# Seven-product pairs spread through each half of the down projection, post-norm transposes moved two kept tiles back, left operands built one block sooner

## The chip, the cores and the metric

The kernel runs on one core of a Trainium2 chip. The metric is the device time of one execution in microseconds (us), compared as the median of several runs. TensorE (PE in the tables) multiplies; VectorE (DVE) and ScalarE (ACT) prepare its operands; GpSimd (POOL) computes a few small things; SyncE (SP) issues nearly all weight loads.

## The reference

One layer of a decoder on an input `x` of 256 x 2048 in float32:

```python
h = x + 1/2 * post1(SwiGLU_1(pre1(x)))
u = pre_m(h);  p = u @ W_in          # S5 input, attention q/k/v, gates
h = h + post_m((sigmoid(g_A) * y_A + sigmoid(g_B) * y_B) @ W_out)
h = h + 1/2 * post2(SwiGLU_2(pre2(h)))

def _swiglu(x, wg, wu, wd):          # 2048 -> 5632 -> 2048
    return (jax.nn.silu(x @ wg) * (x @ wu)) @ wd
```

`pre` and `post` are RMS norms with a gain. `y_A` is a state-space branch, `y_B` a sparse attention. The change touches the two SwiGLU blocks, ffn1 and ffn2, and the norm behind ffn1.

## The kernel before

**Split products.** Every float32 operand is written as `hi + lo`, both rounded to the format that TensorE takes, and a product is three matmuls: hi by hi, lo by hi, hi by lo (lines 523 to 525; 278 to 280 in the plain blocks). A matmul is 128 x 128 by 128 x 512.

**Weight stream.** `Stream` loads weights as tiles of 128 x 1024 (512 KB): SP issues the load into one of `RAW_BUFS = 5` buffers (line 94), ACT makes `hi` (line 103), DVE makes `lo` (line 105). When DVE has made `lo`, the buffer is free and SP can issue the load five tiles on. DVE executes its instructions in program order.

**Seven-product pairs.** For some pairs of weight tiles, x and y, a 2 x 2 block product is done with seven products in place of eight (`fast_pair`): 21 matmuls in place of 24. DVE forms sums of x and y first: line 134 needs both tiles landed and writes the first half of `sums`, line 139 and line 140 write the second half. Then four operands are split: x itself, half of y (`ah0` in the down projection), the first half of the sums, and the second half. The last one is called *the last lo* here; its `lo` is read by the last product group of the pair. Line 139 of the next pair overwrites what the last lo reads.

**Left operands.** The activations have to be combined too (`fast_left_act`, lines 486 to 497: four sums, four differences, four splits of 128 x 384), once for ffn1, before block 5, and once for ffn2, before block 1, where the first seven-product blocks begin.

**Down projection.** `project` runs two halves of 1024 output columns. Within a half, `DOWN_MAIN` lists the order of the 18 pairs of weight tiles; 8 to 13 are seven-product pairs (`DOWN_FAST`), the others are plain pairs of 24 matmuls. Half 0 ends with pairs 18 to 21. In half 1 these four are kept: their eight split tiles stay in the buffer, are multiplied with the first 128 tokens (t = 0), then the post-norm of t = 0 runs (sum line 575, square line 390, scale line 400, power on POOL line 402, gain line 404, residual line 419, transposes line 322), and meanwhile the eight kept tiles are multiplied with the other 128 tokens (t = 1). `ORDER` places the transposes of t = 0 among these: before which kept tile stands which group.

```python
DOWN_FAST = (8, 9, 10, 11, 12, 13)
DOWN_MAIN = [0, 1, 2, 3, 8, 4, 9, 5, 6, 10, 7, 11, 14, 15, 12, 16, 13, 17]
ORDER = {3: 1, 4: 2, 5: 3}   # kept tile number: group of transposes
```

Of the kernel before, what the change touches and what calls it, by code (L numbers as in the profile page):

```python
# [22 lines left out]
KD = D // 128  # L23
# [11 lines left out]


DOWN_FAST = (8, 9, 10, 11, 12, 13)
DOWN_MAIN = [0, 1, 2, 3, 8, 4, 9, 5, 6, 10, 7, 11, 14, 15, 12, 16, 13, 17]
DOWN_ORDER = (DOWN_MAIN + [18, 19, 20, 21], DOWN_MAIN)
DOWN_KEPT = (18, 19, 20, 21)  # L40
RAW_BUFS = 5
# [6 lines left out]

EARLY_GATES = 3
OPENING = [(0, 0), 1, 2, (0, 1), (1, 0), 3, (0, 2), (1, 1), 4, (0, 3), (1, 2), (1, 3)]  # L50
ORDER = {3: 1, 4: 2, 5: 3}
MAGIC = 12582912.0
LN2_HI = 0.693359375
LN2_LO = -2.12194440e-4
# [119 lines left out]
def body(tc, a):  # L174
# [70 lines left out]
    stream = Stream(tc, st, items)  # L245
# [17 lines left out]
    background = []  # L263

    def pump(n=1):
        for _ in range(n):
            if background:
                background.pop(0)()

    def block(lhs, nk, width=512, tick=None, held=0, between=None, behind=None, lag=0):  # L270
        acc = [ps.tile([128, 512], F32, name="acc", tag="acc") for _ in range(NT)]

        def products(parts, kk, t):
            wh, wl = parts
            for k in range(wh.shape[1]):
                lh, ll = lhs(t, kk + k)
                o = acc[t][:, :width]
                T.matmul(o, lh, wh[:, k, :], start=kk + k == 0, stop=False)  # L278
                T.matmul(o, lh, wl[:, k, :], start=False, stop=False)  # L279
                last_product[0] = T.matmul(o, ll, wh[:, k, :], start=False, stop=kk + k == nk - 1).ins  # L280

        kk = 0
        kept = []
        late = []
        while kk < nk:
            parts = stream.next()
            products(parts, kk, 0)
            if kk < nk - held:
                late.append((parts, kk))
                if len(late) > lag:  # L290
                    products(*late.pop(0), 1)
            else:
                kept.append((parts, kk))
                if late:
                    products(*late.pop(0), 1)
            kk += parts[0].shape[1]
            if tick is not None:
                tick(kk)
        for x in late:
            products(*x, 1)  # L300
        if held:
            if between is not None:
                between(acc)
            for n, (parts, k0) in enumerate(kept):
                ins = behind(n) if behind is not None else None
                with tc.issue_after(ins) if ins is not None else nullcontext():
                    products(parts, k0, 1)
        return acc
# [126 lines left out]
    def project_plain(lhs, nk, post, held, tick=None):  # L435
        for nb in range(NBD):
# [5 lines left out]
            else:  # L442
# [7 lines left out]
                def behind(n):  # L450
                    c = ORDER.get(n)
                    return post.moved[0][c] if c is not None and post.moved[0] else None
# [46 lines left out]
    def fast_left_act(pool):  # L499
        step = 2 * (FAST_PAIRS[1] - FAST_PAIRS[0])  # L500

        def part(t, j):
            ks = slice(2 * FAST_PAIRS[0] + j, 2 * FAST_PAIRS[-1] + j + 1, step)
            return act_h[t][:, ks], act_l[t][:, ks]

        n = len(FAST_PAIRS)
        h, l = (pool.tile([128, 4, n, 128], F32R, name=nm) for nm in ("sh", "sl"))
        fast_left([(0, n, part)], lambda j, i, n: (h[:, j, i:i + n], l[:, j, i:i + n]))
        return lambda j, i: (h[:, j, i], l[:, j, i])
# [110 lines left out]
    def ffn(name, rr, gen, post, last, tables=False):  # L620
        g0 = first_block(name, gen) if gen is not None else opening(name)
        pools = []

        def open_pool(nm):
            pools.append(tc.tile_pool(name=nm, bufs=1, reuse_waits="tile"))
            return pools[-1].__enter__()

        hp = first_pool = open_pool("hTa")
        pre = [None]
        if tables:  # L630
            pre[0] = tc.tile_pool(name="pre", bufs=1, reuse_waits="tile")
            with tc.issue_after(stream.rounded[9]):
                s5_tables(pre[0].__enter__())
        hT = []
        pend = []

        def tick(kk):
            if kk == 8 and pend:
                pend.pop()()
            pump(1 + (kk % 8 == 0))  # L640

        def finish(nb, hs):
            def f():
                nonlocal hp
                if nb == 8:
                    hp = open_pool("hTb")
                x = hp.tile([128, NT, 2, 4, 128], F32R, name="hT", tag="hT", bufs=3 if nb >= 8 else 8)
                hT.append(x)
                for t in range(NT):
                    p = transpose4(hs[t])  # L650
                    S.activation(x[:, t, 0], p, AF.Copy)
                    V.tensor_tensor(x[:, t, 1], p, x[:, t, 0].bitcast(F32), op=ALU.subtract)
            return f

        fast = FAST_BLOCKS["ffn1" if tables else "ffn2"]
        left = None
        for nb in range(NBF):
            if nb in fast:
                if left is None:
                    if pre[0] is not None:  # L660
                        pump(len(background))
                        pre[0].__exit__(None, None, None)
                    fp = tc.tile_pool(name="fast", bufs=1, reuse_waits="tile")
                    stream.sums_pool = fp.__enter__()
                    left = fast_left_act(stream.sums_pool)

                def after(nb=nb):
                    if nb == fast[-1]:
                        fp.__exit__(None, None, None)
                        stream.sums_pool = None  # L670
                    if pend:
                        pend.pop()()

                banks = (xp, ps) if (nb - fast[0]) % 2 == 0 else (ps, xp)
                spare[0] = banks[1]
                g, u = both(left, *banks, after)
                spare[0] = xp
            else:
                g = g0 if nb == 0 else block(act, KD, tick=tick)
                u = block(act, KD, tick=lambda kk: pump(1 + (kk % 8 == 0)))  # L680
            hs = []
            for t in range(NT):
                sg = work()
                h = work()
                S.activation(sg, g[t], AF.Silu, scale=rr(t))
                V.scalar_tensor_tensor(h, u[t], rr(t), sg, op0=ALU.mult, op1=ALU.mult)
                hs.append(h)
            pend.append(finish(nb, hs))

        def lhs(t, kk):  # L690
            x = hT[kk // 4]
            return x[:, t, 0, kk % 4, :], x[:, t, 1, kk % 4, :]

        stream.alloc[last] = lambda: first_pool.tile(
            [128, NT, 2, 4, 128], F32R, name="hT", tag="hT", bufs=8).rearrange("p t h k c -> p (t h k c)")

        spaces = [ap_.tile([128, KD, 128], F32R, name=n, tag=n) for n in ("ah0", "al0", "ah1", "al1")]
        sums = spaces[1].bitcast(F32).rearrange("p (j k) c -> p j (k c)", j=4)
        stream.sums_pool = Spaces(spaces[0][:, :8].rearrange("p (j k) c -> p j (k c)", j=2), sums)
        n0 = DOWN_FAST[0] // 2  # L700

        def source(i, n):
            x = hT[n0 + i // 2]
            ks = lambda j: slice(2 * (i % 2) + j, 2 * (i % 2) + 2 * n, 2)
            return i, n, lambda t, j: (x[:, t, 0, ks(j)], x[:, t, 1, ks(j)])

        def place(j, i, n):
            if j == 2:  # L710
                return source(i, n)[2](1, 0)
            j = min(j, 2)
            if i == 5:
                return spaces[0][:, 8 + j:9 + j], spaces[0][:, 11 + j:12 + j]
            return tuple(x[:, 3 * i + j:3 * i + 3 * n - 2 + j:3] for x in spaces[2:])

        def dleft(j, i):
            return tuple(x[:, 0] for x in place(j, i, 1))

        gp = open_pool("gain")  # L720
        fast_left([source(0, 2)], place)
        gen2 = project(lhs, DOWN_ORDER, DOWN_KEPT, DOWN_FAST, dleft, post, (xp, ps), gp,
                       ({2: pend.pop(), 4: lambda: fast_left([source(2, 2)], place),
                         6: lambda: fast_left([source(4, 1), source(5, 1)], place)}, {}))
        stream.sums_pool = None
        for p in reversed(pools):
            p.__exit__(None, None, None)
        return gen2
# [755 lines left out]
```

## Time and profile before

| what | value |
|---|---|
| median of 3 runs | 2120.59 us (2119.51 to 2121.81) |
| profiled execution: its time, its span | 2119.69 us, 2117.9 us |
| outside the span | 1.8 us |
| PE busy | 2099.0 us, 99% of the span |
| DVE busy, ACT busy | 1576.2 us (74%), 1116.1 us (53%) |
| PE on the chain that ended last | 97% |

PE is the engine that sets the time, so the table of its few waits is the place to look for what can be won, and the slack between DVE and PE is the place to look for what can be lost.

### The profile page before, as it was taken

To read this page: it belongs to the slowest core of one execution; us is meant where nothing else is said; L and a number is where in the kernel's file an instruction comes from. 1 tells how busy PE (TensorE), PEld (TensorE's weight loads), DVE (VectorE), ACT (ScalarE), POOL (GpSimd) and SP (SyncE) were. 2 spreads that over 40 slices of the span, in tenths; PEclk is the share of its full clock that TensorE was granted. 3 is DMA by queue.
4 is the path that set the end of the run, shared out by engine and by line. 5 is a ranking of instruction groups with operands and counts; after the bars stand their busy time and mean duration, and the time that the engine had idled before them with its cause. 6 is when DMAs were issued, how large, how long until landed. Compare 5 with 4: busy or idle time off the path is not lost.

```text
span 2117.9 us, 27939 instructions
## 1 busy us (share of the span) xinstructions
PE 2099.0 (99%) x10048; PEld 1729.1 (82%) x10048; DVE 1576.2 (74%) x2268; ACT 1116.1 (53%) x1537; POOL 269.0 (13%) x494
## 2 busy tenths in 40 slices
PE   8999999999999999999999999999999999999998
PEld 7888788888888788998787778888888888888886
DVE  7998898986867864455466656567998899778676
ACT  6444455554555565554445554465555555555453
POOL 1222200000000002993104320000000000000000
PEclk9999999999999999999999999999999999999999
DMA  8877666665665756567854346675666665656665
GB/s 285 269 244 248 191 207 206 193 217 173 215 208 192 271 194 224 166 217 257 276 164 139 123 144 211 209 268 166 212 189 195 201 210 181 218 170 209 218 208 179
DMA packets 137146, 437.63 MB, mean 207 GB/s; under 512 B 14880, under 2 KB 27312, under 8 KB 136880
## 3 DMA queue, kind: packets, MB, share of 16 engines
q1 hardware_dynamic: 117504, 403.10, 59.1%
q10 hardware_dynamic: 19504, 32.75, 4.6%
q8 instruction: 79, 1.29, 0.2%
q14 instruction: 59, 0.48, 0.1%
HBM read 417.42 MB, written 21.52 MB: 207 GB/s over the span
## 4 chain that ended last, share of the span: by engine, by line
PE 97%; DMA 1%; issue 1%; DVE 0%; ACT 0%; POOL 0%; DVEq 0%; SPq 0%; POOLq 0%; ACTq 0%
PE bank L523 16%; PE bank L524 16%; PE bank L525 16%; PE acc L278 14%; PE acc L279 14%; PE acc L280 14%; PE xp L322 2%; PE xp L1262 1%; PE xp L989 1%; DMA raw<-in_w_in 1%; PE xp L1250 1%; PE xp L1012 1%; PE xp L1151 0%; PE xp L1226 0%; PE xp L1227 0%
## 5 line engine op out<-in xcount | busy, mean ns | idle before, releaser
L105 DVE TENSOR_TENSOR lo<-raw,hi 128x1024 fp32r<-128x1024 f32 (+3 forms) x676 | 797.4, 1190 | 353.5 <-ACT hi L103 343.4
L103 ACT ACTIVATE hi<-raw 128x1024 fp32r<-128x1024 f32 (+3 forms) x676 | 685.6, 1023 | 635.8 <-PE acc L280 340.6
L278 PE MATMUL acc<-hi,ah 128*128 128x512 f32 (+2 forms) x1072 | 415.3, 389 | 1.9 <-ACT hi L103 1.9
L279 PE MATMUL acc<-lo,ah 128*128 128x512 f32 (+2 forms) x1072 | 414.4, 387 | 0.0
L280 PE MATMUL acc<-hi,al 128*128 128x512 f32 (+2 forms) x1072 | 413.1, 386 | 0.0
L524 PE MATMUL bank<-lo,ah 128*128 128x512 f32 x758 | 296.8, 392 | 0.0
L525 PE MATMUL bank<-hi,al 128*128 128x512 f32 x746 | 290.9, 390 | 0.0
L523 PE MATMUL bank<-hi,ah 128*128 128x512 f32 x758 | 274.6, 392 | 1.0 <-ACT hi L103 1.0
L278 PEld LDWEIGHTS acc<-hi,ah 128*128 128x128 f32 x1072 | 201.6, 188 | 42.6 <-ACT hi L103 2.7
L279 PEld LDWEIGHTS acc<-lo,ah 128*128 128x128 f32 x1072 | 201.8, 188 | 38.6 <-issue 1.9
L280 PEld LDWEIGHTS acc<-hi,al 128*128 128x128 f32 x1072 | 201.7, 188 | 37.9 <-issue 0.2
L524 PE MATMUL bank<-lo,hT 128*128 128x512 f32 x520 | 202.7, 390 | 0.0
L525 PE MATMUL bank<-hi,hT 128*128 128x512 f32 x520 | 202.6, 390 | 0.0
L523 PE MATMUL bank<-hi,hT 128*128 128x512 f32 x520 | 191.0, 390 | 0.1
L523 PEld LDWEIGHTS bank<-hi,ah 128*128 128x128 f32 x758 | 141.3, 188 | 31.8 <-ACT hi L103 3.4
L524 PEld LDWEIGHTS bank<-lo,ah 128*128 128x128 f32 x758 | 142.4, 188 | 29.6
L525 PEld LDWEIGHTS bank<-hi,al 128*128 128x128 f32 x746 | 140.2, 188 | 28.7
L103 ACT ACTIVATE hi<-sums 128x1024 fp32r<-128x1024 f32 x84 | 89.0, 1059 | 125.8 <-DVE sums L140 109.4
L105 DVE TENSOR_TENSOR lo<-sums,hi 128x1024 fp32r<-128x1024 f32 x84 | 102.8, 1224 | 35.0 <-ACT hi L103 35.0
L523 PEld LDWEIGHTS bank<-hi,hT 128*128 128x128 f32 x520 | 97.5, 188 | 20.9 <-ACT hi L103 0.9
L525 PEld LDWEIGHTS bank<-hi,hT 128*128 128x128 f32 x520 | 97.6, 188 | 20.3
L524 PEld LDWEIGHTS bank<-lo,hT 128*128 128x128 f32 x520 | 97.7, 188 | 20.2
(322 smaller groups left out, 2679.6 us busy)
## 6 DMA issues: line engine op xcount, KB each, us to landing
raw<-in_ffn_gu SPq DMA_DIRECT2D x352, 512.0 KB, 4.1
raw<-in_ffn_d SPq DMA_DIRECT2D x176, 512.0 KB, 4.3
raw<-in_w_ya SPq DMA_DIRECT2D x64, 512.0 KB, 3.5
raw<-in_w_in SPq DMA_DIRECT2D x40, 512.0 KB, 4.3
raw<-in_w_gate_b SPq DMA_DIRECT2D x32, 512.0 KB, 4.2
raw<-in_w_out SPq DMA_DIRECT2D x32, 512.0 KB, 4.1
raw<-in_w_o SPq DMA_DIRECT2D x16, 512.0 KB, 3.7
tab<-s5out ACTq DMA_DIRECT2D x8, 768.0 KB, 5.9
```

What stands on the lines that cost most here:

```text
L103: self.rounded.append(nc.scalar.activation(h, r, AF.Copy).ins)
L105: self.rest = nc.vector.tensor_tensor(l, r, h.bitcast(F32), op=ALU.subtract).ins
L278: T.matmul(o, lh, wh[:, k, :], start=kk + k == 0, stop=False)
L279: T.matmul(o, lh, wl[:, k, :], start=False, stop=False)
L280: last_product[0] = T.matmul(o, ll, wh[:, k, :], start=False, stop=kk + k == nk - 1).ins
L322: last_transpose[0] = T.transpose(p[:, k, :], src[:, k * cols:(k + 1) * cols], ident).ins
L523: T.matmul(out, lh, wh[:, j, :], start=key not in self.started, stop=False)
L524: T.matmul(out, lh, wl[:, j, :], start=False, stop=False)
L525: last_product[0] = T.matmul(out, ll, wh[:, j, :], start=False, stop=last).ins
L989: T.matmul(sp[:, r, q, :], bt[:, r, q, :], urel[:, ct, q, :], start=True, stop=True)
L1012: T.matmul(yps[-1][64 * q2:64 * q2 + 64, ct % 2, qh, :], st8[:, r, 4 * ct + q, 0:64] if r < 2 else urel[:, ct, q, :], tab[:, r, q, :], sta ...
L1250: T.transpose(p[:, b, kb, :], PP[:, hf, b, kb * 128:(kb + 1) * 128], ident)
```

## The change

Three edits. `DOWN_MAIN` now alternates seven-product and plain pairs one by one. `ORDER` puts the transposes before kept tiles 5, 6 and 7 in place of 3, 4 and 5; the mixer's output projection reads the same table. The left operands of the first seven-product block are built in the up product of the block ahead of it, at its fifth step (`kk == 4`), not at the block's own start.

```diff
-DOWN_MAIN = [0, 1, 2, 3, 8, 4, 9, 5, 6, 10, 7, 11, 14, 15, 12, 16, 13, 17]
+DOWN_MAIN = [0, 1, 2, 3, 8, 4, 9, 5, 10, 6, 11, 7, 12, 14, 13, 15, 16, 17]
-ORDER = {3: 1, 4: 2, 5: 3}
+ORDER = {5: 1, 6: 2, 7: 3}
@@ ffn
-                if left is None:
-                    if pre[0] is not None:
-                        pump(len(background))
-                        pre[0].__exit__(None, None, None)
-                    fp = tc.tile_pool(name="fast", bufs=1, reuse_waits="tile")
-                    stream.sums_pool = fp.__enter__()
-                    left = fast_left_act(stream.sums_pool)
...
-                u = block(act, KD, tick=lambda kk: pump(1 + (kk % 8 == 0)))
+                def tick_u(kk, nb=nb):
+                    nonlocal left, fp
+                    pump(1 + (kk % 8 == 0))
+                    if nb + 1 == fast[0] and kk == 4:
+                        if pre[0] is not None:
+                            pump(len(background))
+                            pre[0].__exit__(None, None, None)
+                        fp = tc.tile_pool(name="fast", bufs=1, reuse_waits="tile")
+                        stream.sums_pool = fp.__enter__()
+                        left = fast_left_act(stream.sums_pool)
+
+                u = block(act, KD, tick=tick_u)
```

Both programs have the same instructions, only in another order. On DVE, in half 0 of ffn1's down projection, behind pair 8 (its last lo reads `al0_4724`, where the sums lie), before:

```order
755 L140 TENSOR_TENSOR al0_4724<-al0_4724,raw_4896 128x512
756 L105 TENSOR_TENSOR lo_5059<-al0_4724,hi_5058 128x1024
757 L105 TENSOR_TENSOR lo_5069<-raw_4955,hi_5068 128x1024
758 L105 TENSOR_TENSOR lo_5078<-raw_4967,hi_5077 128x1024
759 L105 TENSOR_TENSOR lo_5088<-raw_4980,hi_5087 128x1024
760 L105 TENSOR_TENSOR lo_5100<-raw_4998,hi_5099 128x1024
761 L134 TENSOR_TENSOR al0_4724<-raw_5056,raw_5072 128x1024
```

and now:

```order
755 L140 TENSOR_TENSOR al0_4724<-al0_4724,raw_4896 128x512
756 L134 TENSOR_TENSOR al0_4724<-raw_4980,raw_4998 128x1024
757 L105 TENSOR_TENSOR lo_5057<-al0_4724,hi_5056 128x1024
758 L105 TENSOR_TENSOR lo_5067<-raw_4955,hi_5066 128x1024
759 L139 TENSOR_TENSOR al0_4724<-al0_4724,raw_4980 128x512
760 L105 TENSOR_TENSOR lo_5076<-raw_4967,hi_5075 128x1024
761 L105 TENSOR_TENSOR lo_5089<-raw_4980,hi_5088 128x1024
```

The tiles raw_4980 and raw_4998 were two plain tiles and are now a seven-product pair, so line 134, which needs both landed, stands ahead of the last lo of the pair before (lo_5059, now lo_5057), where nothing stood.

In half 1 of the same projection, on DVE from the first place where the two orders differ, before:

```order
841 L105 TENSOR_TENSOR lo_5906<-al0_4724,hi_5905 128x1024
842 L105 TENSOR_TENSOR lo_5924<-al0_4724,hi_5923 128x1024
843 L105 TENSOR_TENSOR lo_5934<-raw_5860,hi_5933 128x1024
844 L105 TENSOR_TENSOR lo_5943<-raw_5872,hi_5942 128x1024
845 L105 TENSOR_TENSOR lo_5953<-raw_5885,hi_5952 128x1024
846 L134 TENSOR_TENSOR al0_4724<-raw_5921,raw_5937 128x1024
847 L105 TENSOR_TENSOR lo_5965<-raw_5903,hi_5964 128x1024
```

and now, one whole turn of a seven-product pair and a plain pair:

```order
842 L134 TENSOR_TENSOR al0_4724<-raw_5885,raw_5903 128x1024
843 L105 TENSOR_TENSOR lo_5922<-al0_4724,hi_5921 128x1024
844 L139 TENSOR_TENSOR al0_4724<-al0_4724,raw_5885 128x512
845 L105 TENSOR_TENSOR lo_5932<-raw_5860,hi_5931 128x1024
846 L140 TENSOR_TENSOR al0_4724<-al0_4724,raw_5903 128x512
847 L105 TENSOR_TENSOR lo_5941<-raw_5872,hi_5940 128x1024
848 L105 TENSOR_TENSOR lo_5954<-raw_5885,hi_5953 128x1024
849 L105 TENSOR_TENSOR ah0_4723<-raw_5903,ah0_4723 128x512
850 L105 TENSOR_TENSOR lo_5984<-al0_4724,hi_5983 128x1024
851 L134 TENSOR_TENSOR al0_4724<-raw_5963,raw_5981 128x1024
852 L105 TENSOR_TENSOR lo_6000<-al0_4724,hi_5999 128x1024
```

Again line 134 has moved ahead of a last lo (lo_5924, now lo_5922), and in this half it does so in two turns running; raw_5981 is loaded into the buffer that lo_5954 frees.

On PE, at the end of ffn1, the place of the transposes of t = 0 (xp), before:

```order
3113 L524 MATMUL bank_5696<-hT_6375,hT_4826 128x512
3114 L525 MATMUL bank_5696<-hT_6375,hT_4826 128x512
3115 L322 MATMUL xp_6509<-ident_75,wk_5485 128x128 x4
3116 L322 MATMUL xp_6524<-ident_75,wk_5487 128x128 x4
3117 L523 MATMUL bank_5696<-hT_6400,hT_4826 128x512
```

and now:

```order
3125 L524 MATMUL bank_5697<-hT_6411,hT_4482 128x512
3126 L525 MATMUL bank_5697<-hT_6411,hT_4482 128x512
3127 L322 MATMUL xp_6509<-ident_75,wk_5413 128x128 x4
3128 L322 MATMUL xp_6524<-ident_75,wk_5415 128x128 x4
3129 L523 MATMUL bank_5697<-hT_6422,hT_4482 128x512
3130 L322 MATMUL xp_6539<-ident_75,wk_6278 128x128 x4
3131 L322 MATMUL xp_6554<-ident_75,wk_6280 128x128 x4
```

The transposes stand two kept tiles (twelve matmuls) later, and the third and fourth group follow the first two with one matmul between.

## Rows read from the trace of the kernel before

**Rows 1.** The page: busy time, share of the span and instructions of each engine.

```profile
PE 2099.0 (99%) x10048; PEld 1729.1 (82%) x10048; DVE 1576.2 (74%) x2268; ACT 1116.1 (53%) x1537; POOL 269.0 (13%) x494
```

**Rows 2.** A wait of PE in the whole span: total us, times, longest.

```profile
PE bank L523 <- ACT hi L103: 1.0, 4, 0.3
```

**Rows 3.** Timeline of PE, block 5 of ffn1: start, length, instruction, idle before.

```profile
260.79 0.39 PE L524 MATMUL bank<-lo,sh 128*128 128x512 f32 x1
261.47 0.51 PE L523 MATMUL bank<-hi,ah 128*128 128x512 f32 x1 [0.29 <-ACT hi L103]
261.81 0.39 PE L525 MATMUL bank<-hi,sl 128*128 128x512 f32 x1
...
264.15 0.40 PE L525 MATMUL bank<-hi,al 128*128 128x512 f32 x1
```

**Rows 4.** Timelines of PE, DVE and POOL at ffn1's post-norm.

```profile
732.71 0.39 PE L525 MATMUL bank<-hT 128*128 128x512 f32 x1
735.15 1.78 PE L322 MATMUL xp<-ident,wk 128*128 128x128 f32 x8 [2.05 <-DVE wk L419]
...
731.34 0.68 DVE L575 TENSOR_TENSOR wk<-bank,wk 128x512 f32<-128x512 f32 x1
...
734.34 1.42 DVE L419 SCALAR_TENSOR_TENSOR wk<-wk,rpa 128x512 f32<-128x512 f32 x2 [0.46 <-POOL rpa L402]
```

**Rows 5.** Windows: PE, PEld, DVE, ACT, POOL busy (instructions), PE clock, DMA share, GB/s.

```profile
205.00:247.00 42.00, 42.00 (x214) 34.11 (x213) 30.12 (x48) 18.01 (x20) 14.60 (x32) 1.00 0.73 229
1416.00:1440.00 24.00, 24.00 (x108) 19.88 (x107) 9.95 (x11) 10.12 (x10) 0.00 (x0) 1.00 0.45 151
735.20:739.00 3.80, 3.80 (x14) 3.09 (x15) 2.50 (x5) 3.64 (x12) 0.00 (x0) 0.55 0.97 356
```

**Rows 6.** Timeline of DVE: four full-wide lo behind each other.

```profile
544.28 4.63 DVE L105 TENSOR_TENSOR lo<-raw,hi 128x1024 fp32r<-128x1024 f32 x4
```

**Rows 7.** Timeline of PE: first product with the last lo, in the four halves.

```profile
544.56 0.39 PE L524 MATMUL bank<-lo,ah 128*128 128x512 f32 x1
...
659.05 0.39 PE L524 MATMUL bank<-lo,hT 128*128 128x512 f32 x1
...
659.96 0.39 PE L524 MATMUL bank<-lo,ah 128*128 128x512 f32 x1
...
1913.81 0.39 PE L524 MATMUL bank<-lo,ah 128*128 128x512 f32 x1
...
2029.20 0.39 PE L524 MATMUL bank<-lo,ah 128*128 128x512 f32 x1
```

**Rows 8.** Single loads: when SP issued them, and us to landing.

```profile
L94 SPq DMA_DIRECT2D raw<-in_ffn_d x1: 327/327/327, 539.0 to 539.0; - x1
DMA to landing us min/median/max: 4.7/4.7/4.7
...
L94 SPq DMA_DIRECT2D raw<-in_ffn_d x1: 446/446/446, 653.3 to 653.3; - x1
DMA to landing us min/median/max: 4.8/4.8/4.8
...
L94 SPq DMA_DIRECT2D raw<-in_ffn_d x1: 328/328/328, 1908.2 to 1908.2; - x1
DMA to landing us min/median/max: 4.5/4.5/4.5
...
L94 SPq DMA_DIRECT2D raw<-in_ffn_d x1: 327/327/327, 2022.2 to 2022.2; - x1
DMA to landing us min/median/max: 4.9/4.9/4.9
```

**Rows 9.** All weight loads of half 0 and of half 1: us to landing.

```profile
DMA to landing us min/median/max: 3.4/4.4/5.5
...
DMA to landing us min/median/max: 3.3/4.5/6.0
```

**Rows 10.** Waits for loads in the seven-product blocks of ffn1, 262 to 440 us.

```profile
  DVE sums L134: 1.8, 2
```

More of the change, by code (lines that the diff above doesn't have):

```diff
@@ L655, in ffn @@
         fast = FAST_BLOCKS["ffn1" if tables else "ffn2"]
-        left = None
+        left = fp = None
         for nb in range(NBF):
             if nb in fast:
-                if left is None:
-                    if pre[0] is not None:
-                        pump(len(background))
-                        pre[0].__exit__(None, None, None)
-                    fp = tc.tile_pool(name="fast", bufs=1, reuse_waits="tile")
-                    stream.sums_pool = fp.__enter__()
-                    left = fast_left_act(stream.sums_pool)
                 def after(nb=nb):
```

## The prediction

> **What bounds the kernel now.** I read the busy times first: PE works in 99% of the span [rows 1], so the time changes only by work taken off PE, which this change doesn't do, by waits of PE, or by its clock. The list of PE's waits and the starts of its matmuls then show what there is to win: a new matmul starts every 0.227 us when nothing is late (659.05 to 659.96 is four of them) [rows 7].
>
> Three places lose time that the change speaks to. In block 5 of ffn1, 8 steps of PE take from 260.79 to 264.15, 3.36 us, where 8 x 0.227 = 1.81 would do: 1.55 us lost, because ACT's hi comes late [rows 3]. The list counts four such waits, two here and two in block 1 of ffn2, so I take 1.55 us twice [rows 2]. At ffn1's post-norm the last kept product of the first stretch starts at 732.71 and the first transpose at 735.15, 2.44 us where 0.23 would do: 2.21 us [rows 4]. Behind it PE ran at a mean clock of 0.55, so at the lower of its two levels, 1.2 GHz, nearly throughout 735.2 to 739 [rows 5]; that costs (1 - 0.55) x 3.8 = 1.7 us more. All told 1.55 + 1.55 + 2.2 + 1.7 = 7.0 us.
>
> **The left operands.** The four sums, four differences and four low parts (twelve DVE instructions, about 0.55 us each) and ACT's four splits move one block ahead. They are some 6 us of DVE. From 205 to 247, where they now fall, DVE is busy 30.12 of 42 us, and from 1416 to 1440 for ffn2 9.95 of 24 [rows 5]: 12 and 14 us are free, so they fit, and DVE and ACT no longer have them in front of the splits that PE waits for. I take both 1.55 us as won. If they only half fit, the bounds are 0 and 3.1 us.
>
> **The transposes.** Before, three kept tiles (18 matmuls) lay behind the last t = 0 product of the row sum; now five do. Two tiles are 12 x 0.227 = 2.72 us of cover; the wait was 2.2 us [rows 4]. Of the chain, the last sum (line 575, at 731.34) came late behind a lo and the chain from it to line 419 took 3.0 us; in the new order the lo stands earlier and the loads of the residual are issued before the kept tiles' loads, so the chain starts no later. Cover exceeds need by 0.5 us at least, and with no idle there is nothing to halve the clock: 3.9 us won. The later transposes delay the next projection's first products by nothing that the cover doesn't hold; at the mixer PE waits for no transpose before, and I put the edit there at nothing.
>
> **The pairs.** Moving them removes no work. What moves is line 134: on DVE it now waits for the second tile of the next pair, ahead of the last lo of the present pair, and everything on DVE queues behind it. PE reads that lo in its next products. So the last lo is ready one line 134 and one lo behind the landing: 1.14 + 1.22 [rows 6], with 0.1 for the signals 2.5 us. Until there nothing has moved, so the landing times of before hold. The four halves [rows 7, 8]:
>
> ffn1 half 0: issued 539.0, landed 543.7, lo ready 546.2, read at 544.56: 1.65 us late.
> ffn1 half 1: 653.3, 658.1, 660.6, read at 659.96: 0.65 us late.
> ffn2 half 0: 1908.2, 1912.7, 1915.25, read at 1913.81: 1.45 us late.
> ffn2 half 1: 2022.2, 2027.1, 2029.65, read at 2029.20: 0.45 us late.
>
> This repeats, because pairs now alternate. A turn of a seven-product pair and a plain pair is 45 matmuls, 10.2 us of PE. On DVE, where a last lo stands behind line 134, the turn is, from line 134's start: last lo at 1.1, line 139 at 2.4, a plain lo at 3.0, line 140 at 4.1, a second plain lo at 4.7, the lo of x at 5.9, done at 7.1 (full-wide 1.14 us apart, half-wide about half). Only then is x's buffer free, and SP issues the next pair's second tile into it. I price its landing at 4.5 us, the median of the loads in these halves (3.3 to 6.0 [rows 9]); there are others in flight 1 and 3 us ahead of it, so the lone load's 3.4 is too short and 4.8 the other end. With 0.1 the turn is 11.75 us, 1.55 over PE's. In the second place of half 1 this comes on top in full: 0.65 + 1.55 = 2.2 us late. Where the last lo stands ahead of line 134, the turn is 10.5 to 10.6 us and what comes late is the first plain lo, by 0.2 to 0.5 us. Carried through in this way, half 0 of ffn1 loses 1.65 + 0.25 = 1.9, half 1 loses 0.65 + 1.55 + 0.45 + 0.4 = 3.05; ffn2 1.45 + 0.25 = 1.7 and 0.45 + 1.55 + 0.45 + 0.4 = 2.85. That is 9.5 us in some 12 waits; and the matmul behind a wait starts 0.34 us, not 0.23, after the last (261.47 to 261.81) [rows 3], so 12 x 0.11 = 1.3 more. Loss 10.8 us. With a landing of 3.4 in the later turns it would be 1.65 + 1.2 + 1.45 + 1.0 and 6 waits, 6.0 us; with 4.8 about 14.
>
> The Trainium skill, page "DMA: Bandwidth & Descriptors", section "Anatomy of one DMA — SWDGE (gpsimd) path", gives a load as about 2.0 us plus its bytes over 436 GB/s. By it 512 KB would land in 3.2 us, an estimate, and the loss would be about 5.5 us; the loads here come from SP's queue, and their shortest of 3.3 and median of 4.4 to 4.5 [rows 9] are what the sum uses.
>
> **The sum.** 10.8 - 7.0 = 3.8 us over the profiled execution's 2119.69: 2123.5. That execution was 0.9 us below the median of the three runs, so on the median it is 2124.4 us, 0.18% up. A measurement of this kernel tells some 0.2% (4.2 us) from no change, so this is just within.
>
> **The rivals.**
> The clock falls too. The one idle of PE that was followed by the lower clock was 2.05 us [rows 4]; those of 0.3 us in block 5 were not. The new ones of 1.45 to 1.65 us, one in each half, lie between, and nearer to the first. One fall costs 1.7 us, but DVE's turn catches up meanwhile, so that later waits in that half vanish: net 1.5 in half 0, 0.9 in half 1. All four: 4.8 us on top, 2129.2; one or two: 2126. The Trainium skill, page "TensorE: Matmul & The Clock Gate", section "HAM oscillation — how this bites in real kernels", tells of a loop whose matmuls wait for a load in each turn and lose the clock in each turn; the fall at 735 us is a case of it here, but after one wait and with 2.05 us of idle.
>
> Only the first waits count: the later second tiles land like lone loads, in 3.4 us. Loss 6.0, 2119.6 us on the median, no change.
>
> Faster: no new wait of weight. The seven-product blocks of ffn1 alternate in the same way, and there line 134 waited twice, 1.8 us in all, in 180 us [rows 10], without PE. Against it: there line 134 stands behind the last lo and one plain lo. It decides at the landing: if each second tile, the first ones too, landed in 3.4 us, the first waits would be 0.35 and 0.3 us, the others none, and nearly the whole 7.0 us were won: 2114.3 us. No load that counts was that fast.
>
> The change does little of what it says: the left operands meet other work and the 3.1 us stay: 2127.
>
> **How the numbers follow.** Forecast 0.47, with its own range 2121.5 to 2127 (landings of 4.1 to 4.8 us). Clock 0.25, first waits only 0.13, faster 0.11, operands late 0.04. Slower by over 0.2% is the clock's 0.25, a third of the forecast's and the last case's 0.04, less a little: 0.42. Faster 0.11, and the rest 0.47. The range holds 8 in 10 only with one of the two ends; since both have weight I go from 2114 to 2129.
>
> **What would show it.** Right: waits of PE for DVE's lo in the down projections, at about 543, 657, 668 us and their like in ffn2, the first some 1.6 us; DVE's line 134 idle before it, released by a load; no wait in block 5 of ffn1 and block 1 of ffn2; no idle and no lower clock at the transposes. Wrong: lower clock behind those waits (the clock's rival), waits in the second turns below 1 us (short landings), or a transposes' wait that is only moved.

## The result and the profile after

The changed kernel is slower by more than the prediction's whole range allowed: median 2133.86 us of six runs (2129.38 to 2138.06), beside 2121.78 us for the kernel before (six runs on the same chip), ratio 1.0059 with a 95% interval of 1.0044 to 1.0073. That is 12.1 us, where 3.8 were forecast. The profiled execution of the changed kernel took 2138.06 us (span 2136.2) and was the slowest of its six; that of before, 2119.69 us, was on the quick side of its own. Between the two traces there are thus 18.4 us to be placed, and the account below is made for these; the medians are accounted for separately at the end.

The busy line of the page answers to [rows 1]:

```profile
PE 2102.0 (98%) x10048; PEld 1727.5 (81%) x10048; DVE 1571.7 (74%) x2268; ACT 1115.7 (52%) x1537; POOL 272.2 (13%) x494
```

The work is the same; what grew is waiting. The list of PE's waits in the changed kernel (line waited on, total us, times, longest) holds three rows that the one of before doesn't have: the first, the fourth and the last one below. The row of [rows 2] and the wait for line 419 are gone from it:

```profile
PE bank L524 <- DVE lo L105: 15.1, 14, 2.4
PE xp L322 <- DMA wk<-in_x: 5.3, 2, 5.1
PE acc L278 <- ACT hi L103: 1.9, 2, 1.4
PE xp L322 <- DVE bd L862: 1.9, 1, 1.9
PE xp L1017 <- POOL st L1005: 1.2, 1, 1.2
```

The same matmul can be looked up in both traces; the difference of its two start times says how far the changed kernel has fallen behind by then. The places where this difference jumps give the account (us, worked out from the starts of PE's rows in the two traces):

```
place (us in the trace before)              forecast   measured
start of the kernel                            0         +0.56
226: transposes line 322 wait for bd           0         +2.16
262-268: block 5 of ffn1                      -1.55      -1.35
272, 314, 402: ffn1's seven-product blocks     0         +3.77
ffn1 half 0: four waits                       +1.9       +5.44
ffn1 half 1: a wait and the clock behind it   +3.05      +4.40
735-746: transposes of the post-norm          -3.9       -3.95
973: line 1017 waits for POOL                  0         +1.30
1463: block 1 of ffn2                         -1.55      -1.57
ffn2 half 0: two waits                        +1.7       +2.89
ffn2 half 1: four waits                       +2.85      +4.52
```

The rows sum to 18.2 us; the forecast for the halves had 1.3 us more for restarts, spread over its waits.

The three gains came out to within 0.2 us. PE's timeline in the changed kernel shows the transposes starting 0.23 us behind the kept product, where [rows 4] had 2.44 us, and a window over them (columns as in [rows 5]) has the full clock, where that had 0.55:

```profile
750.54 0.39 PE L525 MATMUL bank<-hT 128*128 128x512 f32 x1
750.77 1.03 PE L322 MATMUL xp<-ident,wk 128*128 128x128 f32 x8
```

```profile
748.00:752.00 4.00, 4.00 (x24) 3.38 (x24) 3.45 (x9) 3.66 (x12) 0.42 (x1) 1.00 0.73 255
```

The losses came where the prediction put them, and larger. In half 0 of ffn1 PE's timeline has four of them (in brackets the idle time ahead and what ended it), where a first of 1.65 us and small ones of 0.25 us together were forecast:

```profile
551.29 0.50 PE L524 MATMUL bank<-lo,ah 128*128 128x512 f32 x1 [1.46 <-DVE lo L105]
...
563.65 0.50 PE L524 MATMUL bank<-lo,hT 128*128 128x512 f32 x1 [0.26 <-DVE lo L105]
...
575.78 0.50 PE L524 MATMUL bank<-lo,hT 128*128 128x512 f32 x1 [1.63 <-DVE lo L105]
...
587.01 0.50 PE L524 MATMUL bank<-lo,hT 128*128 128x512 f32 x1 [0.95 <-DVE lo L105]
```

On DVE, in half 1, the cause stands as the prediction described it: line 134 sits idle until a load lands, and the last lo (`lo<-al,hi`) is queued directly behind it. Between two such stops DVE does its whole turn in one run:

```profile
668.14 1.23 DVE L134 TENSOR_TENSOR al<-raw 128x1024 f32<-128x1024 f32 x1 [3.28 <-DMA raw<-in_ffn_d]
669.28 1.22 DVE L105 TENSOR_TENSOR lo<-al,hi 128x1024 fp32r<-128x1024 f32 x1
670.54 0.69 DVE L139 TENSOR_TENSOR al<-al,raw 128x512 f32<-128x512 f32 x1
...
675.76 1.21 DVE L105 TENSOR_TENSOR lo<-al,hi 128x1024 fp32r<-128x1024 f32 x1
681.08 1.23 DVE L134 TENSOR_TENSOR al<-raw 128x1024 f32<-128x1024 f32 x1 [4.11 <-DMA raw<-in_ffn_d]
682.23 1.22 DVE L105 TENSOR_TENSOR lo<-al,hi 128x1024 fp32r<-128x1024 f32 x1
```

The run frees four buffers in 3.5 us, so SP issues four loads close together, at 575.8, 577.5, 578.6 and 579.2 in half 0. The first is alone and takes 3.5 us; the third is the second tile y that line 134 waits for; the fourth takes longest. Three views of SP's loads of that turn: all four, the third and the fourth.

```profile
L94 SPq DMA_DIRECT2D raw<-in_ffn_d x4: 328/328/328, 575.8 to 579.2; - x4
...
DMA to landing us min/median/max: 3.5/5.2/6.5
...
L94 SPq DMA_DIRECT2D raw<-in_ffn_d x1: 328/328/328, 578.6 to 578.6; - x1
...
DMA to landing us min/median/max: 5.8/5.8/5.8
...
L94 SPq DMA_DIRECT2D raw<-in_ffn_d x1: 328/328/328, 579.2 to 579.2; - x1
...
DMA to landing us min/median/max: 6.5/6.5/6.5
```

So y lands 5.8 us after its issue, not 4.5; line 134 is late, DVE's next run is bunched again, and the burst repeats itself. From one line 134 to the next, half 0 takes 12.36, 11.40 and 11.96 us (548.88, 561.24, 572.64, 584.60), where PE needs 10.2 and the prediction had 10.5 to 10.6 for this half.

What the prediction had no term for is the stretch at 226 us, ahead of block 5, where the left operands now lie. Rows of POOL, DVE, ACT and PE of the changed kernel there:

```profile
212.53 6.80 POOL L892 COPY hz<-hs 32x32 f32<-32x32 f32 x1 [13.95 <-DVE hs L887]
...
219.18 1.28 DVE L652 TENSOR_TENSOR hT<-xp,hT 128x512 fp32r<-128x512 f32 x2
...
224.50 2.01 ACT L103 ACTIVATE hi<-raw 128x1024 fp32r<-128x1024 f32 x2 [7.99 <-POOL hz L892]
...
225.59 1.22 DVE L105 TENSOR_TENSOR lo<-raw,hi 128x1024 fp32r<-128x1024 f32 x1 [4.80 <-ACT hi L103]
...
228.10 0.63 PE L322 MATMUL xp<-ident,bd 128*128 128x128 f32 x4 [1.89 <-DVE bd L862]
```

A tiny copy of 32 x 32 on POOL takes 6.80 us. In the trace of before the same copy takes 0.51:

```profile
208.78 0.51 POOL L887 COPY hz<-hs 32x32 f32<-32x32 f32 x1 [14.67 <-DVE hs L882]
```

It is the first of sixteen such copies, and ACT issues the DMA that sends out their result behind the last of them. All sixteen and that issue, first in the changed kernel, then before:

```profile
212.53 11.48 POOL L892 COPY hz<-hs 32x32 f32<-32x32 f32 x16 [13.95 <-DVE hs L887]
...
224.04 0.34 ACTq L896 DMA_DIRECT2D s5out<-hz  x1
...
208.78 8.70 POOL L887 COPY hz<-hs 32x32 f32<-32x32 f32 x16 [14.67 <-DVE hs L882]
...
217.51 0.34 ACTq L891 DMA_DIRECT2D s5out<-hz  x1
```

So ACT issues it 6.5 us later. Only 2.8 us of these are the longer copies; the other 3.75 us are their later start: they wait for line 887 on DVE, which now stands behind work of the left operands (the whole kernel was 0.6 us behind by then). ACT stands 7.99 us in front of this DMA, its next hi comes late, DVE waits 4.80 us for that hi, and PE's transposes wait 1.89 us for DVE.

### The profile page after: what moved, and what is told of

It reads as the page before. It is cut to its first block, busy times and chain, and to the rows that moved or that the text cites. A ratio compares the mean times of both kernels' runs of the same rounds, so it can differ in the third digit from the quotient of the medians.

```text
span 2136.2 us, 27921 instructions
## 1 busy us (share of the span) xinstructions
PE 2102.0 (98%) x10048; PEld 1727.5 (81%) x10048; DVE 1571.7 (74%) x2268; ACT 1115.7 (52%) x1537; POOL 272.2 (13%) x494
## 4 chain that ended last, share of the span: by engine, by line
PE 74%; DVE 9%; POOL 7%; DMA 5%; issue 3%; ACT 1%; DVEq 0%; SPq 0%; ACTq 0%; POOLq 0%
PE bank L524 12%; PE bank L525 11%; PE acc L278 11%; PE acc L279 11%; PE acc L280 11%; PE bank L523 11%; DVE lo L105 5%; DMA raw<-in_ffn_d 4%; PE xp L322 2%; POOL st L1005 2%; POOL sc L1002 2%; POOL sc L1003 1%; POOL st L1004 1%; DMA raw<-in_ffn_gu 1%; POOL hz L892 1%
## 5 line engine op out<-in xcount | busy, mean ns | idle before, releaser
L105 DVE TENSOR_TENSOR lo<-raw,hi 128x1024 fp32r<-128x1024 f32 (+3 forms) x676 | 797.3, 1186 | 349.5 <-ACT hi L103 345.1
L524 PE MATMUL bank<-lo,ah 128*128 128x512 f32 x758 | 297.6, 393 | 9.6 <-DVE lo L105 9.6
L523 PE MATMUL bank<-hi,ah 128*128 128x512 f32 x758 | 281.4, 391 | 0.0
L524 PE MATMUL bank<-lo,hT 128*128 128x512 f32 x520 | 203.8, 392 | 5.5 <-DVE lo L105 5.5
L524 PEld LDWEIGHTS bank<-lo,ah 128*128 128x128 f32 x758 | 142.4, 188 | 42.5 <-DVE lo L105 13.9
L524 PEld LDWEIGHTS bank<-lo,hT 128*128 128x128 f32 x520 | 98.0, 188 | 28.8 <-DVE lo L105 8.6
L105 DVE TENSOR_TENSOR lo<-sums,hi 128x1024 fp32r<-128x1024 f32 x84 | 101.0, 1216 | 5.1 <-ACT hi L103 4.3
```

What stands on the lines that cost most here:

```text
L105: self.rest = nc.vector.tensor_tensor(l, r, h.bitcast(F32), op=ALU.subtract).ins
L523: T.matmul(out, lh, wh[:, j, :], start=key not in self.started, stop=False)
L524: T.matmul(out, lh, wl[:, j, :], start=False, stop=False)
```

## The experiments

Each experiment was timed beside the kernel before, whose median lay between 2121.3 and 2121.9 us throughout.

**ORDER alone, pairs alone, left operands alone.** Three kernels each make one of the three edits of the diff: its line of `ORDER`, its line of `DOWN_MAIN`, its piece in `ffn`. The expectations:

> Only the transposes' table is changed, the other two edits are left as before. Theory (the five-tile cover hides the whole chain of the post-norm): no wait at ffn1's transposes, no lower clock behind them, 3.9 us less than before, ratio about 0.998. Rival (with the DVE order of before, line 575 still comes late behind a lo, and the wait is only moved to the fifth kept tile): at most 1 us won, ratio 0.9995 or more, and a wait of PE for line 419 stays in the list.

> Only the order of the pairs in the down projections is changed. Theory (the alternating pairs alone make the last lo late, by landings of 5 to 6 us of each pair's second tile): 10 to 17 us more than before, ratio 1.005 to 1.008, some ten waits of PE for DVE's lo in the four halves, none before 530 us; the profiled runs of one kernel differ by several us. Rival (the halves are late because the left operands' edit has pushed the loads and DVE out of step): under 5 us, ratio below 1.0025.

> Only the left operands are built one block sooner, in both ffn. Theory (in ffn1 the twelve DVE instructions meet the state-space tables' work, hold up GpSimd's copies and with them ACT's queue, and the seven-product blocks then run with late loads; in ffn2 nothing is in the way): ffn1 2 to 5 us slower, ffn2 1.5 us faster, together 1 to 3.5 us more than before, ratio 1.0005 to 1.0015. Rival (the wait at 226 us and those at 272 to 403 us in the changed kernel are accidents of one execution): both ffn win 1.5 us, 3 us less than before, ratio 0.9986.

Measured: ORDER alone 2117.71 us (2116.75 to 2119.78), ratio 0.9987 [0.9978, 0.9996]. The transposes start right behind their kept product, at the full clock; the mechanism and its 3.9 us (PE's starts move by 2.21, 1.24 and 0.45 us) are confirmed.

The pairs alone: 2132.06 us (2129.63 to 2135.5), ratio 1.0061 [1.0047, 1.0074], as its theory had it. That is 10.75 us, most of the 12.1 us that the whole change lost. Its list of PE's waits has the row

```profile
PE bank L524 <- DVE lo L105: 9.4, 8, 1.6
```

and PE's starts in the four halves fall behind by some 12.6 us in all (3.4, 2.6, 3.5 and 3.1). But this kernel, with the old ORDER, has no wait at the transposes either: they start 0.23 us behind their kept product,

```profile
738.43 0.39 PE L525 MATMUL bank<-hT 128*128 128x512 f32 x1
738.66 1.32 PE L322 MATMUL xp<-ident,wk 128*128 128x128 f32 x8
```

and 3.6 us come back there. Measured against PE's products the last sum (line 575) ran 1.9 us sooner: it started at 735.11, where 731.34 of before and the 5.7 us lost until then would make 737.05. That the plain pairs at the end of a half bring this about is read from the order; it was not tried apart from the time that PE had lost before. Two of the three edits thus win nearly the same 3.9 us.

The left operands alone: 2119.78 us (2116.32 to 2123.07), ratio 0.9993 [0.9984, 1.0001]. Neither expectation came: the theory had it 1 to 3.5 us slower, the rival 3 us faster, the medians say 1.5 us faster, and the interval includes no change. Its profiled execution, the slowest of eleven at 2123.07, has the copy of 6.80 us, PE's wait behind it and a loss in the seven-product blocks again, and was 4.5 us behind at 460 us; the others probably lost less there, but no trace shows them.

**Additivity.** The pairs and ORDER together, left operands as before:

```diff
-DOWN_MAIN = [0, 1, 2, 3, 8, 4, 9, 5, 6, 10, 7, 11, 14, 15, 12, 16, 13, 17]
+DOWN_MAIN = [0, 1, 2, 3, 8, 4, 9, 5, 10, 6, 11, 7, 12, 14, 13, 15, 16, 17]
-ORDER = {3: 1, 4: 2, 5: 3}
+ORDER = {5: 1, 6: 2, 7: 3}
```

> Edit: the new order of pairs and the transposes behind the last three tiles, left operands as before. Theory (the new order of pairs alone already takes the transposes' wait away, so ORDER adds nothing to it): like e2_down, 2130.5 to 2133 us. Rival (the gains add up): e2_down's 2132.1 us less ORDER's own 3.6 us, 2127.5 to 2129.5 us.

Measured 2131.23 us (2130.66 to 2132.82), ratio 1.0048 [1.0036, 1.0060]: the theory's case. ORDER, worth 3.6 us alone, gives about 1 us beside the new pairs (0.8 by the medians, 1.2 with each taken against its own runs of before), and the two intervals overlap, so it may be nothing.

**Line 134 in another queue place.** The whole change stays, and line 134 is put behind the last lo of the pair before, in the seven-product blocks as well as in the halves:

```diff
-            V.tensor_tensor(self.sums[:, 0:2], x, y[:, 1:2].to_broadcast([128, 2, 512]), op=ALU.add)
+            with self.behind(self.last_lo):
+                V.tensor_tensor(self.sums[:, 0:2], x, y[:, 1:2].to_broadcast([128, 2, 512]), op=ALU.add)
...
+            if kind == 3:
+                self.last_lo = self.rest
```

> Edit: all of the change stays, but line 134 (the sum that waits for the second tile y) is put behind the last lo of the seven-product pair before it. Theory (the loss in the four down halves comes from line 134 standing ahead of a last lo, not from seven-product and plain pairs taking turns): the waits L524 <- DVE lo of 1.0 to 1.6 us in the halves go, and with them what the pairs cost alone, 12.25 us by the shift in e2_down's trace; the gain at the transposes stays, so 2118 to 2121 us. Rival (the loads come too late in bursts whatever the order, so that the wait passes to the next lo or to line 134's successors): waits of L524 of at least 0.5 us remain at half of the places or more, 2125 to 2130 us.

Measured 2118.59 us (2117.53 to 2121.38), ratio 0.9991 [0.9982, 1.0000]. One line of the program in another queue place gives back 15.3 us of the changed kernel's time, pairs in turns and all. By PE's starts most of it comes from the halves (2.3 us lost there, where the changed kernel's trace had 17.25) and a part from the seven-product blocks, where the line was moved too (1.1 us, not 3.8). PE's waits (the lines have moved by one to four; L528 is the old L524, L106 the old L105):

```profile
PE bank L528 <- DVE lo L106: 2.0, 6, 0.5
```

In half 0 the line, now 136, doesn't wait at all, and of the four loads of a turn the last is issued 2.4 us behind y, not 0.6. All four, and y alone:

```profile
L95 SPq DMA_DIRECT2D raw<-in_ffn_d x4: 328/328/328, 556.7 to 562.0; - x4
...
DMA to landing us min/median/max: 3.5/3.8/4.5
...
L95 SPq DMA_DIRECT2D raw<-in_ffn_d x1: 328/328/328, 559.6 to 559.6; - x1
...
DMA to landing us min/median/max: 4.1/4.1/4.1
```

In half 1 of ffn1 the bursts stay, y lands in 4.9 to 5.8 us and line 136 idles 1.0 to 3.1 us, but PE loses at most 0.4 us at a place, since no last lo is queued behind it. So it takes both, the late landing and the lo behind it, and the queue place decides.

**The left operands of ffn1.** Sooner in ffn1 alone (`and tables` in the condition); and the same with DVE's share queued behind its newest split, which takes it out of the stretch from 205 to 220 us:

```diff
-                    if nb + 1 == fast[0] and kk == 4:
+                    if nb + 1 == fast[0] and kk == 4 and tables:
...
-                        left = fast_left_act(stream.sums_pool)
+                        with stream.behind(stream.rest):
+                            left = fast_left_act(stream.sums_pool)
```

> Edit: the kernel before with the left operands sooner in ffn1 alone. Theory (the GpSimd copy at line 892 stands still while VectorE works without a gap through the left operands): copy of about 6.8 us, a wait of about 1.9 us of the transposes at line 322 for bd at 226 us, further waits L524 <- DVE lo near 272 us, against 1.4 us gained at block 5: 2121 to 2123.5 us, thus same or slower. Rival (those waits are only of the profiled execution): the gain of 1.4 us alone counts, 2119 to 2120.5 us.

> Edit: as e7_left1, but VectorE's share of the left operands is queued behind its newest split, so that it no longer lies in the stretch from 205 to 220 us. Theory (copy held up by VectorE's unbroken work): the copy at line 892 takes under 1 us, no wait of line 322 for bd at 226 us, block 5 still starts 1.4 us sooner, 2118.5 to 2120.5 us. Rival (the copy is held up by something else, such as its data or the post-norm's DMA): copy again over 5 us, the wait at 226 us stays, 2121 to 2123.5 us.

Measured 2122.13 us (2118.10 to 2125.29) and 2120.47 us (2118.60 to 2121.79), ratios 1.0005 [0.9997, 1.0014] and 0.9997 [0.9989, 1.0006]. Each median is where the theory put it, but the two intervals overlap; what tells them apart is the trace. The first has the copy at 6.80 us, a wait of 0.7 us for bd and one of 1.7 us at 274 us. The second has the copy at 0.51 us, no wait for bd, and 0.4 us as its longest wait for a lo.

Then the same question within the whole change: first with DVE's share of ffn1's left operands behind the newest split (`with stream.behind(stream.rest if tables else None):`), then with ffn1's left operands at their old place and only ffn2's sooner (`and not tables` in the condition):

> Edit: the whole change as it is, only VectorE's share of ffn1's left operands queued behind its newest split. Theory (what the sooner left operands cost comes from VectorE's unbroken stretch at 205 to 220 us and the copy at line 892 that stands still in it): copy under 1 us, no wait of line 322 for bd near 226 us of more than 0.6 us, 2128.5 to 2131.5 us, thus 1 to 1.5 us for each ffn below e13_down_order's 2131.2 us or level with it, and the runs within 4 us of each other. Rival (in the combination the left operands cost something else): still 2132.5 to 2135 us, with runs over 6 us apart.

> Edit: the whole change, but with ffn1's left operands at their old place; only ffn2's are sooner. Theory (all the cost lies in ffn1): e13_down_order's 2131.2 us less the 0.9 us that ffn2's gave in e4_best against e1_order, 2129.5 to 2131 us, runs within 4 us. Rival (ffn2's share costs too, or the spread comes from the pairs): 2132 to 2135 us.

Measured 2129.20 us (2126.89 to 2132.09) and 2130.67 us (2128.94 to 2133.54), ratios 1.0039 [1.0025, 1.0053] and 1.0044 [1.0031, 1.0056]. Both fall below the changed kernel's 2133.86, by 4.7 and 3.2 us, though their intervals overlap with its 1.0044 to 1.0073. The copy is short in both; in the first it also starts 3.6 us sooner than in the changed kernel:

```profile
208.94 0.51 POOL L893 COPY hz<-hs 32x32 f32<-32x32 f32 x1 [11.14 <-DVE hs L888]
```

The spread, 4.6 and 5.2 us, is a little more than the 4 us expected.

**Better versions.** The kernel before with ORDER and the left operands sooner in ffn2 alone; then the same with ffn1's sooner too, DVE's share behind the newest split; last the whole change with both queue places mended. The lines that differ from the kernel before in the second:

```diff
-ORDER = {3: 1, 4: 2, 5: 3}
+ORDER = {5: 1, 6: 2, 7: 3}
...
+                    if nb + 1 == fast[0] and kk == 4:
...
+                        with stream.behind(stream.rest if tables else None):
+                            left = fast_left_act(stream.sums_pool)
```

> The transposes' table as changed, the left operands sooner in ffn2 alone, the pairs in the order of before. Theory (the edits' parts add up): 3.9 + 1.5 = 5.4 us less than before, ratio 0.9974, no wait of PE at ffn1's transposes or in block 1 of ffn2, those in block 5 of ffn1 as before. Rival (an earlier arrival at the later loops turns into waits there, as in ffn1): 3 us or less, ratio above 0.9985.

> Edit: the pairs as before, transposes behind the last three tiles, left operands sooner in ffn2 and, with VectorE's share queued behind its newest split, in ffn1. Theory: e4_best (2116.8 us) less the 1.4 us at ffn1's block 5 that e4_best leaves: 2115.0 to 2116.3 us. Rival (the sooner left operands take VectorE's lead from the seven-product blocks behind, waits L524 <- DVE lo at 272 us as in the changed kernel): 2117 to 2120 us.

> Edit: the whole change, with line 134 put behind the last lo of the pair before (as e5_behind) and VectorE's share of ffn1's left operands queued behind its newest split (as e10_best2). Theory (these two queue places are all that the change lost): copy at line 892 under 1 us, no wait of line 322 for bd near 226 us, no wait above 0.6 us in the down halves; e5_behind's 2118.6 us less about 1.4 us: 2116 to 2118 us, thus not below e10_best2 with the old order of pairs. Rival (taking turns is worth something by itself once its waits are gone): below 2114.5 us.

Measured 2116.79 us (2115.99 to 2117.75), 2115.06 us (2113.43 to 2119.43) and 2118.34 us (2115.73 to 2124.70); ratios 0.9982 [0.9973, 0.9990], 0.9975 [0.9965, 0.9984] and 0.9986 [0.9977, 0.9994]. The first lies between its theory (0.9974) and its rival (0.9985), and its interval holds both; as the theory had it, PE's waits at the transposes and in block 1 of ffn2 are gone. The second has the lowest median of the study, 6.4 us under the kernel before and where its theory put it, but its interval overlaps with the first's; its profiled execution, the slowest of eight at 2119.43, has the rival's waits, 0.46 us at 272.5 and 0.80 at 315.6. The third has the pairs in turns almost without their waits. It came out 0.3 us above its theory's 2116 to 2118, with a wait of 0.71 us in half 1 of ffn1, where 0.6 was the bound, and one of 1.51 us at 314.7 in the seven-product blocks. It is no faster than ORDER alone, so nothing shows that the new order of pairs wins anything by itself. Nor did the short copy win anything here: 2118.34 us with it, 2118.59 with the copy of 6.80 us, which the kernel with only line 134 moved still has.

## Why the prediction was wrong

Right were the bound (PE, by its waits), the three gains in size and place, and the place and mechanism of the loss (line 134 ahead of a last lo). Of the first waits those of the two halves 0 were right, forecast 1.65 and 1.45 us, measured 1.74 and 1.41; those of the two halves 1, forecast 0.65 and 0.45, were 0.11 and 0.81, and the two errors partly cancel. Two steps failed.

**The landing of the later second tiles.** "I price its landing at 4.5 us, the median of the loads in these halves" is the mis-sized term. In the changed kernel y landed in 4.2 to 5.8 us, 5.4 to 5.8 in the later turns of half 0. The median of before was taken from loads of a DVE that worked evenly; behind a stop of 2 to 4 us DVE frees four buffers in a row, and a load is issued 0.6 us behind y's. Over the 336 landings of second tiles in the down projections of all fourteen traces, sorted by the time to the next load's issue: median 4.8 us (3.9 to 6.1, 96 loads) where that was under 0.7 us, and 3.6 us (3.4 to 4.9, 42 loads) where it was over 2.6. In the kernel with line 134 moved the load ahead of y's was issued 1.74 us before it in the later turns of both halves, and mainly the one behind differs: 2.4 us after it in halves 0, where y landed in 3.5 to 4.5 us, and 0.6 us in halves 1, where it took 4.2 to 5.8. So the load close behind goes with the later landing; how the two slow each other no run shows. The sentence that followed from it, a turn of 10.5 to 10.6 us and 0.2 to 0.5 us lost where the last lo stands ahead of line 134, cost 3.7 us in half 0 of ffn1 alone (0.53 + 1.91 + 1.26), against 0.25. All told the halves lost 17.25 us in the profiled execution, against 10.8; in the two kernels that have the new pairs without the sooner left operands some 12.6 and 13.3.

**The left operands of ffn1.** "12 and 14 us are free, so they fit" and its bounds of 0 to 3.1 us left out a loss. Free time of DVE was not what mattered: with the left operands DVE worked from 205 to 220.8 us without a gap, line 887 on DVE ran late, the copies behind it took longer, and ACT and DVE waited for each other behind them. 2.16 us were lost there, and 3.77 us in the seven-product blocks behind, against 1.35 gained. These are figures of the slowest of six executions. By the medians ffn1's share cost 3.2 us (2133.86 less 2130.67) and ffn2's gave 0.6 (2131.23 less 2130.67); the intervals of the three ratios overlap, so both are estimates. The 3.2 us also belong to this kernel only: in the kernel before, ffn1's share changed the median by 0.7 us (2122.13 beside 2121.44, an interval that includes no change). Why the same edit costs more beside the new pairs stays open.

On the copy the Trainium skill, page "SBUF — State Buffer", section "SBUF: two separate sides", says that the port pair which GpSimd and VectorE share "is an **exclusive lock**, not a bandwidth split", held for a whole instruction, by VectorE too where it reads two operands from SBUF. The traces agree in how the copy ends: in all four kernels where it took 6.80 us it ended 0.15 us after DVE began line 652 (219.33 and 219.18 above), the first instruction in that run with a large operand from PSUM. They don't say why it found no gap earlier: at the same instructions of DVE (the sum into bd and the small copies behind it) it got through in 0.51 us in the kernel before. That it goes with the left operands' place on DVE is shown: the four kernels with ffn1's share sooner and not queued behind the newest split have it, the other ten don't. The step within is argued. Nor does the long copy set the size of the loss: PE's wait for bd behind it was 1.89, 1.86, 0.74 and 0.56 us in these four.

**The sum.** The gains were added as if each edit had its own wait to remove. ORDER's 3.9 us and the pairs' end of a half are one wait, but since both edits are in the change this cost the sum nothing; it misleads only who keeps one of them. The medians split the change into steps, each kernel less the one with an edit fewer: pairs and ORDER +9.55 us (2131.23 less 2121.68) where 10.8 less 3.9 gave 6.9; ffn2's left operands -0.6 where -1.55 was forecast; ffn1's +3.2 where -1.55 was. The steps add up to the measured loss by construction, so this checks nothing, and the interval of each ratio is 5 to 6 us wide. As an estimate, ffn1's left operands are the larger part of the miss, 4.75 of 8.3 us, and the pairs 2.65.

Of the rivals, the one of the clock came true once: behind the idle of 2.37 us at 683.5 the window has half the clock, which costs 1.5 us in these 3.0 us. Columns are PE, PEld, DVE, ACT, POOL busy, clock, DMA share, GB/s:

```profile
680.74:684.90 4.16, 1.79 (x8) 1.14 (x7) 3.78 (x4) 1.72 (x3) 0.00 (x0) 0.97 0.06 26
684.90:687.90 3.00, 3.00 (x9) 2.35 (x8) 3.00 (x4) 0.88 (x1) 0.00 (x0) 0.50 0.44 131
```

Behind the idles of 1.46, 1.63 and 1.89 us the clock stayed at 1.00, so one fall came, not four. The rival judged a fall by the length of the idle, and length alone doesn't decide it. In the kernel with the left operands alone an idle of 1.92 us was followed by half the clock, and one of 2.07 us, at the transposes, by the full one:

```profile
274.13 0.50 PE L524 MATMUL bank<-lo,ah 128*128 128x512 f32 x1 [1.92 <-DVE lo L105]
...
275.10:278.40 3.30, 3.30 (x9) 2.50 (x9) 3.30 (x5) 0.33 (x1) 0.00 (x0) 0.50 0.69 195
...
739.63 0.55 PE L322 MATMUL xp<-ident,wk 128*128 128x128 f32 x3 [2.07 <-DVE wk L419]
...
739.70:743.00 3.30, 3.30 (x21) 2.68 (x21) 3.02 (x7) 3.30 (x12) 0.00 (x0) 1.00 0.95 365
```

So the 1.7 us of clock within the 3.9 us at the transposes are there to be won only where the clock falls. The case that came true, later landings above 4.8 us together with a loss by ffn1's left operands, was on the list of none of the rivals.

The 1.3 us at 973 belong to no edit. The wait for POOL is missing in the profiled execution of before and stands in those of eleven of the twelve experiments (0.5 to 1.2 us); what brings it about was not tried. Why single executions of some kernels with ffn1's left operands sooner spread by 7 to 9 us stays open too.

## What to carry to other kernels

An instruction that waits for a load is priced by what is queued behind it on its engine: look for the last result that another engine reads soon, and put the waiting instruction behind that one before anything else is reordered. Landing times of a trace hold for the spacing at which its loads were issued; if a change makes the freeing engine stop and run, price the loads as a burst and let the stop repeat. Work that is moved into idle time of an engine can still push back a small step that another engine waits for, so give such a move a bound on the side of loss.

## What was not expected of the hardware

A 32 x 32 copy on POOL took 6.80 us instead of 0.51 beside a run of DVE without gaps, the same 6.80 in four kernels; the group of sixteen that it opens took only 2.8 us longer. Loads of 512 KB that took 3.5 us as the first of a burst took up to 6.5 us as the fourth of four within 3.5 us. PE's clock went to half behind idles of 1.92, 2.05 and 2.37 us, and stayed full behind others of up to 2.07 us.
